# HGRN2 and GLA input blocks in pairs through DRAM, more gate blocks in the mixers, z gates multiplied in the branch stage

## The chip, the cores and the metric

The kernel runs on one core of one Trainium2 chip. The metric is the device time of one execution in microseconds; of the kernel before three runs were timed, and one more execution was profiled. Five engines work side by side: TensorE (PE, with its weight loads PEld), VectorE (DVE), ScalarE (ACT), GpSimd (POOL) and SyncE (SP), which here issues the DMAs.

## The reference

One layer of a hybrid recurrent decoder for 1024 prompt tokens, 16 meta tokens ahead of them, and 8 samples of 4 tokens: 1072 tokens in all, 1056 without the meta tokens.

```python
xn = rmsnorm(h, norm_w)
(gq, gk, gv, glr, gg, hq, hf, hi, hg_g, mq, mk, mv, mi, mf, mo, mg,
 ca, cb, cg, mgate) = split_cols(xn @ w_in)
...
zA = head_rmsnorm(oA, gla_norm) * jax.nn.silu(gg)
...
zB = head_rmsnorm(oB, hg_norm) * jax.nn.silu(hg_g)
...
zC = head_layernorm(hC, ml_norm) * jax.nn.silu(mg)
...
zD = jax.nn.silu(yc32) * jax.nn.silu(cg)
gates = jax.nn.sigmoid(mgate).reshape(Bsz, T, 4, D_MODEL)
mixed = gates[:, :, 0] * (zA @ w_branch[0])
...
h = h + mixed @ w_out
```

`oA` comes from gated linear attention, `oB` from HGRN2 (q is silu(hq), the forget gate f comes from hf, k is 1 - f, v is hi), `hC` from an mLSTM, `yc32` from a causal depthwise convolution over 31 taps and a LayerNorm; `mixed` is the sum over the four branches, and a final RMSNorm ends it. `xn @ w_in` has 1024 input channels and is cut into blocks of 128 output columns; `mgate` alone has 32 of them. Each matrix product is made of three in a shorter format: both operands are split into a high and a low part (`xh`, `xl`, `wh`, `wl`), and high by high, low by high and high by low are added.

## The kernel before, in words

**Stages, with their place in the profiled execution.** Up to about 90 us: the input norm, transposes into `xh` and `xl`, four direct gate blocks (`NDIR`). 90 to 501: the pair stage. 501 to 1300: the mixers, four HGRN2 units (`hg_unit`), two GLA units of two heads each (`gla_unit`) and four mLSTM units (`ml_unit`). 1300 to 1323: two late gate blocks (`LATE`). 1323 to 1517: the branch stage. To the end: `w_out` and the final norm.

**A direct block** (`proj`, `proj_w`, L185 to L187) multiplies one block of 128 columns by all tokens: three groups of tokens (352 wide each without the meta tokens, `GY`; 358, 358 and 356 with them, `GA`), 24 matmuls a group, 72 in all, into an accumulator `acc` from a ring of three. Its weights are loaded by SP (`load_raw`, `wraw`, 512 KB), rounded by ACT into `wh` and subtracted by POOL into `wl` (`split_w`, L138 and L139).

**A pair** (`pair`, L277 to L279) makes two blocks by seven half products in place of eight: the sums and differences of the weights are made on DVE (`ta`, `tb`, L261 to L267), as are two of the splits; the products `sa`, `sb`, `sc`, `sd`, 168 matmuls 268 wide, are added up on ACT and DVE in `p1`, `u2`, `p5` and `u3` (L289 to L310). `pair_to` writes the two blocks to DRAM, after a sigmoid or a silu where one is wanted. The stage has 19 pairs: four that make the conv input (`conv_pair`), and 15 of `todo`: five of gate blocks, two of `cg`, and the eight of `mo`, `gg`, `hg` and `mg`. Each conv pair's 30 taps (`y`, L388) run on DVE under the pairs behind it.

**The mixers** make their own inputs by direct blocks: `hf`, `hq`, `hi` (L185 within `hg_unit`, `vtok`), `gk`, `gq`, `gv`, `mq`, `mk`, `mv`. A unit transposes `v` to tokens (`tta`, `v9p`), makes the decays level by level (`lv`, `tot`), the states (`ds`, `sall`), the outputs (`op`), and in `z_out` transposes the normed output (`zt`) and multiplies it by the norm's weight and the z gate (L720, DVE), which was loaded into `gt` from `sscr`. Sixteen gate blocks (`fill`) are made directly between: two in each HGRN2 unit, one in each GLA unit, one each in three mLSTM units and three in the last.

**The branch stage** takes the branches in the order 1, 0, 2, 3. `load_z` loads four `zr` and splits them on ACT and DVE into `zh` and `zl` (L1149, L1150). For each of eight column blocks `j` the weights `w_br` are loaded and split, 36 matmuls go into three accumulators, DVE multiplies by the gate `gt` and POOL adds to `mix` (L1164, L1165).

**What sets the order.** A list scheduler orders each engine's instructions ahead of time. Each engine goes through its list in order, and so does SP with the DMA issues: an issue that waits for a buffer or for data holds all behind it. Buffers are rings by tag; a tile waits for the readers of the one that it replaces. Pools are opened and closed by stage, so a mixers' tile lies where the pair stage's tiles lay.

Of the kernel before, what the change touches and what calls it, by code (L numbers as in the profile page):

```python
# [65 lines left out]
def trunk(ctx, tc, hx, w_in, w_sm, w_br, w_out, pk, wgk2, mlb, fnorm, s_gla, s_hg, s_c, s_n, s_m, s_cv,  # L66
# [246 lines left out]
    def pair_to(sec, i, dst, func, times=False, base=0):  # L313
# [5 lines left out]
        def c11(s, ps):  # L319
# [4 lines left out]
            if s == 1:  # L324
                DMA.dma_start(dst[i, :, 0:HT - NM], g11[:, NM:])

        def rest(j, second):
            def ev(t):
# [6 lines left out]
                if second:  # L335
                    DMA.dma_start(dst[j, :, HT - NM:], t)
# [233 lines left out]
    def vtok(sec, i, ones_col=False):  # L570
# [4 lines left out]
        def ev(ps, t0, n):  # L575
            S.activation(vf[:, t0:t0 + n], ps, AF.Copy)
# [125 lines left out]
    def z_out(o, rstd, nw, gate, zi, mu=None):  # L702
# [9 lines left out]
        for c0, c1 in QUADS:  # L712
# [7 lines left out]
            V.scalar_tensor_tensor(gate[:, t0:t0 + e - a], ps[:, a:e], nw, gate[:, t0:t0 + e - a], ALU.mult, ALU.mult)  # L720
# [100 lines left out]
    def gla_unit(p):  # L821
# [11 lines left out]
        def ev(ps, t0, n):
            V.tensor_tensor(prod[:, t0:t0 + n], ps, k[:, t0:t0 + n], ALU.mult)
            for i, r in ((0, slice(0, 64)), (1, slice(64, 128))):
                V.tensor_tensor(qg[r, i, t0:t0 + n], ps[r], f[r, t0:t0 + n], ALU.mult)
# [5 lines left out]
        gates = []
        for i in range(2):
            g = tl("gt", [P, NY], 2)
            DMA.dma_start(g, sscr[2 * p + i])
            gates.append(g)
# [486 lines left out]
```

## Time and profile before

| | |
|---|---|
| median of three runs | 1619.72 us (1619.08 to 1622.87) |
| the profiled execution | 1622.92 us |
| its span, from the first to the last instruction | 1621.1 us |
| mean granted clock of TensorE | 0.993 |
| bytes moved by DMA | 176 MB |

A row of the page or of a group gives the line, the engine, the operation, the tile written and those read, the shape and the count; behind the first bar the busy time in us and the mean ns of one; behind the second the idle time just before these instructions and what ended it. A row of the timeline gives start and duration in us, and in brackets the idle time ahead of it and what released it. SPq rows are the issues of DMAs, not the transfers. A row of DMA issues ends with KB and the median us from issue to landing. A row of waits gives the total us, the number and the longest.

### The profile page before, as it was taken

The numbers are of one execution on the slowest core, as the hardware profiler recorded it, in microseconds if no ns is written. First come the engines' busy times: TensorE is split into PE (matmuls) and PEld (weight loads), VectorE is DVE, ScalarE is ACT, GpSimd is POOL, SyncE is SP. The second block draws the span as 40 slices with busy tenths as digits, with TensorE's granted clock in tenths as the row PEclk, the third lists the DMA queues.
The fourth block names the chain that finished last, engine by engine and source line by source line (L and its number), as shares of the span: only waits on it lengthen the run. The fifth ranks groups of instructions, "written<-read, shape, count | busy, mean of one in ns | idle before, by whom it ended". The sixth has DMA issues, their size and how long they took to land.

```text
span 1621.1 us, 27103 instructions
## 1 busy us (share of the span) xinstructions
PE 1582.3 (98%) x10894; PEld 1529.0 (94%) x10894; DVE 1076.6 (66%) x1900; ACT 527.4 (33%) x1015; POOL 467.0 (29%) x412
## 2 busy tenths in 40 slices
PE   7999999899999999999999999999999999999998
PEld 6999999899999999999999998999999999999886
DVE  7959979899994566454544766585864736744523
ACT  6533342333333333212423212133322235522311
POOL 2222222123223122222122322123322312777300
PEclk9999999999999999999999999999999999999999
DMA  5323333232336213131313123143432277676221
GB/s 195 126 75 110 96 105 87 77 103 84 109 99 200 58 38 106 42 101 47 102 46 106 40 68 104 45 147 109 130 96 70 94 222 231 191 232 205 87 105 58
DMA packets 190561, 176.21 MB, mean 109 GB/s; under 512 B 9260, under 2 KB 164800, under 8 KB 190436
## 3 DMA queue, kind: packets, MB, share of 16 engines
q1 hardware_dynamic: 190436, 174.49, 35.1%
q8 instruction: 85, 1.39, 0.4%
q14 instruction: 40, 0.33, 0.1%
HBM read 122.45 MB, written 52.00 MB: 108 GB/s over the span
## 4 chain that ended last, share of the span: by engine, by line
PE 80%; DVE 14%; DMA 2%; issue 2%; ACT 1%; SPq 0%; DVEq 0%; POOLq 0%; POOL 0%; ACTq 0%
PE acc L185 17%; PE acc L187 17%; PE acc L186 17%; DVE y L388 5%; PE lv L627 4%; PE sa L277 2%; PE sa L278 2%; PE sa L279 2%; PE sc L279 1%; PE sc L278 1%; PE sc L277 1%; PE sd L279 1%; PE sd L278 1%; PE sd L277 1%; DVE wl L139 1%
## 5 line engine op out<-in xcount | busy, mean ns | idle before, releaser
L139 POOL TENSOR_TENSOR wl<-wraw,wh 128x1024 fp32r<-128x1024 f32 (+1 forms) x124 | 272.1, 2196 | 680.4 <-ACT wh L138 671.6
L185 PE MATMUL acc<-xh,wh 128*128 128x352 f32 (+2 forms) x1320 | 435.8, 330 | 2.9 <-ACT vt L534 1.9
L186 PE MATMUL acc<-xl,wh 128*128 128x352 f32 (+2 forms) x1320 | 434.3, 329 | 0.0
L187 PE MATMUL acc<-xh,wl 128*128 128x352 f32 (+2 forms) x1320 | 433.5, 328 | 0.0
L185 PEld LDWEIGHTS acc<-xh,wh 128*128 128x128 f32 x1320 | 249.9, 189 | 6.9 <-ACT vt L534 2.9
L186 PEld LDWEIGHTS acc<-xl,wh 128*128 128x128 f32 x1320 | 249.8, 189 | 2.0 <-issue 0.5
L187 PEld LDWEIGHTS acc<-xh,wl 128*128 128x128 f32 x1320 | 249.7, 189 | 1.7 <-issue 0.2
L138 ACT ACTIVATE wh<-wraw 128x512 fp32r<-128x512 f32 (+1 forms) x125 | 110.5, 884 | 253.7 <-PE acc L186 147.7
L388 DVE SCALAR_TENSOR_TENSOR y<-u,pkt,y 128x1024 f32<-128x1024 f32 x120 | 190.8, 1590 | 0.7
L185 PE MATMUL acc<-zh,wh 128*128 128x352 f32 x384 | 124.5, 324 | 0.5 <-DVE gt L1164 0.4
L186 PE MATMUL acc<-zl,wh 128*128 128x352 f32 x384 | 124.3, 324 | 0.0
L187 PE MATMUL acc<-zh,wl 128*128 128x352 f32 x384 | 124.2, 323 | 0.0
L277 PE MATMUL sa<-xh,wh 128*128 128x268 f32 x304 | 89.0, 293 | 6.5 <-ACT u L349 6.1
L642 DVE TENSOR_TENSOR q<-q,tot 128x256 f32<-128x256 f32 (+3 forms) x96 | 59.4, 619 | 53.9 <-PE lv L627 42.6
L278 PE MATMUL sa<-xl,wh 128*128 128x268 f32 x304 | 88.2, 290 | 0.0
L279 PE MATMUL sa<-xh,wl 128*128 128x268 f32 x304 | 88.1, 290 | 0.0
L1165 POOL TENSOR_TENSOR mix<-mix,gt 128x352 f32<-128x352 f32 x72 | 72.1, 1014 | 30.4 <-DVE gt L1164 25.1
L627 PE MATMUL lv<-q,k 128*128 128x128 f32 (+2 forms) x608 | 74.5, 272 | 2.7 <-DVE att L660 2.5
L627 PEld LDWEIGHTS lv<-q,k 128*128 128x128 f32 (+1 forms) x608 | 71.0, 187 | 4.7 <-issue 3.9
L185 PEld LDWEIGHTS acc<-zh,wh 128*128 128x128 f32 x384 | 72.3, 188 | 1.1 <-DVE gt L1164 1.1
L187 PEld LDWEIGHTS acc<-zh,wl 128*128 128x128 f32 x384 | 72.2, 188 | 0.0
L186 PEld LDWEIGHTS acc<-zl,wh 128*128 128x128 f32 x384 | 72.2, 188 | 0.0
(391 smaller groups left out, 3392.9 us busy)
## 6 DMA issues: line engine op xcount, KB each, us to landing
wraw<-w_in SPq DMA_DIRECT2D x92, 512.0 KB, 4.0
gt<-gscr SPq DMA_DIRECT2D x30, 528.0 KB, 5.0
gscr<-gd SPq DMA_DIRECT2D x60, 176.0 KB, 1.9
zr<-zscr SPq DMA_DIRECT2D x16, 528.0 KB
wraw<-w_br SPq DMA_DIRECT2D x32, 256.0 KB, 2.9
gt<-sscr SPq DMA_DIRECT2D x12, 528.0 KB, 3.6
zscr<-gt SPq DMA_DIRECT2D x12, 528.0 KB, 3.3
sscr<-u SPq DMA_DIRECT2D x16, 268.0 KB, 2.3
```

Of the source, the lines that this page charges most:

```text
L138: S.activation(hi[:, :kd], raw[:, :kd], AF.Copy)
L139: (E or G).tensor_tensor(lo[:, :kd], raw[:, :kd], hi[:, :kd], ALU.subtract)
L185: T.matmul(ps, wh(k), ah(k), start=(i == 0), stop=False)
L186: T.matmul(ps, wh(k), al(k), start=False, stop=False)
L187: T.matmul(ps, wl(k), ah(k), start=False, stop=(i == kd - 1))
L277: T.matmul(out, wh, xa[:, k], start=start and k == 0, stop=False, skip_group_check=True)
L278: T.matmul(out, wh, xb[:, k], start=False, stop=False, skip_group_check=True)
L279: T.matmul(out, wl, xa[:, k], start=False, stop=stop and k == KH - 1, skip_group_check=True)
L388: V.scalar_tensor_tensor(ymain, u[:, NM + j:NM + j + NPR], w(j), ymain, ALU.mult, ALU.add)
L627: T.matmul(out(ps[:rows, c], P), k[:, t0:t0 + rows], moving(t0, P), start=True, stop=True)
L642: V.tensor_tensor(qx[:, :, 1], qx[:, :, 1], pv[r, :, 0:1].broadcast_to([rw, nb, h]), ALU.mult)
L1165: G.tensor_tensor(mixed[j][:, t0:t0 + n], mixed[j][:, t0:t0 + n], gt[:, t0:t0 + n], ALU.add)
```

## The change

The 12 blocks of HGRN2 and the 8 of GLA become ten pairs, which write to a new DRAM buffer `pscr`; the units load them back (`take`). The five gate pairs go, and their ten blocks join the fillers: 26 of them, four in every HGRN2 and GLA unit, two in the last mLSTM unit. The loop over the conv pairs takes four pairs of `todo` for each in place of three. `z_out` no longer knows the gate: ACT scales the transposed output by the norm's weight and stores it in pieces, and `load_z` loads the z gate `zg` (one buffer) and multiplies on DVE. `tot` and `sall` get second buffers, and the fillers' output shares `zst` with `z_out`. The raw weights have one buffer in the working pool in place of two; the second raw block of a pair lies in the pair stage's own pool.

```diff
+    pscr = dr.tile([20, P, NT], F32, name="pscr", tag="pscr")
-    def load_raw(src, c0, kd=KD):
-        raw = pools["wp"].tile([P, KD, P], F32, name="wraw", tag="wraw")
+    def load_raw(src, c0, kd=KD, pool="wp"):
+        raw = pools[pool].tile([P, KD, P], F32, name="wraw", tag="wraw", bufs=1)
...
-        r0, r1 = load_raw(w_in, c0), load_raw(w_in, c1)
+        r0, r1 = load_raw(w_in, c0), load_raw(w_in, c1, pool="gph")
...
-    NFILL = 16
-    fill = list(range(32 - NFILL, 32))
-    todo = [("gate", i, gscr, AF.Sigmoid) for i in range(NDIR, 32 - NFILL, 2) if i not in LATE]
+    fill = [j for j in range(NDIR, 32) if j not in LATE]
+    PB, todo, nb = {}, [], 0
+    for sec, n in (("hf", 4), ("hq", 4), ("hi", 4), ("gk", 2), ("gq", 2), ("gv", 4)):
+        PB[sec] = nb
+        todo += [(sec, i, pscr, AF.Copy, False, nb, 0) for i in range(0, n, 2)]
+        nb += n
...
-        pair_to(*todo.pop(0))
+        n = (3, 3, 3, 3)[i]
+        for t in todo[:n]:
+            pair_to(*t)
+        del todo[:n]
...
+    def take(sec, i, dst, lead=0):
+        DMA.dma_start(dst, pscr[PB[sec] + i, :, lead:])
...
-        proj(sec, i, GA, ev)
+        if sec in PB:
+            take(sec, i, vf[:, :NT])
+        else:
+            proj(sec, i, GA, copy_evac(vf))
+        S.activation(x9, vf[:, NP:NT].unsqueeze(1).broadcast_to([P, 3, NT - NP]), AF.Copy)
...
-        tot = tl("tot", [P, 1072], 1)
+        tot = tl("tot", [P, 1072], 2)
...
-            V.scalar_tensor_tensor(gate[:, t0:t0 + e - a], ps[:, a:e], nw, gate[:, t0:t0 + e - a], ALU.mult, ALU.mult)
-        DMA.dma_start(zscr[zi], gate)
+            z = tl("zst", [P, 512], 2)[:, :e - a]
+            S.activation(z, ps[:, a:e], AF.Identity, scale=nw)
+            DMA.dma_start(zscr[zi, :, t0:t0 + e - a], z)
...
-        for _ in range(3 - nh):
+        for _ in range(4):
             filler()
...
-        sall = tl("sall", [P, 9, P], 1)
+        sall = tl("sall", [P, 9, P], 2)
...
-        proj("hf", h, GA, evf)
+        take("hf", h, k)
+        S.activation(f, k, AF.Sigmoid)
+        S.activation(k, k, AF.Sigmoid, scale=-1.0)
+        V.tensor_scalar(f, f, oml[:, h:h + 1], lbA[:, h:h + 1], ALU.mult, ALU.add)
+        V.tensor_scalar(k, k, oml[:, h:h + 1], kb[:, h:h + 1], ALU.mult, ALU.subtract)
         G.memset(q[:, 0:NM], 0.0)
-        proj("hq", h, GY, silu_evac(q))
+        take("hq", h, q[:, NM:], NM)
+        S.activation(q2[:, 1, NM:], q[:, NM:], AF.Sigmoid)
+        V.tensor_tensor(q[:, NM:], q[:, NM:], q2[:, 1, NM:], ALU.mult)
...
-        for _ in range(3 if h == 3 else 1):
+        for _ in range(2 if h == 3 else 0):
             filler()
...
             zr = ztl("zr", 2)
             DMA.dma_start(zr, zscr[4 * b + k])
+            if b < 3:
+                zg = ztl("zg", 1)
+                DMA.dma_start(zg, sscr[4 * b + k])
+                V.tensor_tensor(zr, zr, zg, ALU.mult)
```

**The order on PE between the pair stage and the mixers.** Before: the last product of the last pair (`sd`), then the first direct block, of HGRN2's `hf`.

```order
L277 MATMUL sd_5465<-xh_96,wh_5339 128x268
L278 MATMUL sd_5465<-xl_97,wh_5339 128x268
L279 MATMUL sd_5465<-xh_96,wl_5340 128x268
L185 MATMUL acc_5623<-xh_96,wh_5619 128x358
L186 MATMUL acc_5623<-xl_97,wh_5619 128x358
L187 MATMUL acc_5623<-xh_96,wl_5620 128x358
```

Nine groups of 24 such matmuls stand there before the first `tta`. In the change:

```order
L278 MATMUL sd_6586<-xh_97,wh_6460 128x268
L279 MATMUL sd_6586<-xl_98,wh_6460 128x268
L280 MATMUL sd_6586<-xh_97,wl_6461 128x268
L540 MATMUL tta_6755<-ident_70,vf_6749 128x128 x4
L540 MATMUL tta_6761<-ident_70,vf_6749 128x128 x4
L540 MATMUL tta_6767<-ident_70,vf_6749 48x128
L555 MATMUL v9p_6770<-ident_70,x9_6751 96x128
L186 MATMUL acc_6928<-xh_97,wh_6924 128x352
L187 MATMUL acc_6928<-xl_98,wh_6924 128x352
```

The transposes of `vf`, which is loaded from `pscr`, are next behind the pair; the first direct block, a filler, comes behind them.

**The order on SP at the same place.** Before, the last pair's stores (`u3`, `p1`, `u2`) and what follows them:

```order
L336 DMA sscr_91<-u3_5408 128x536
L338 DMA sscr_91<-p1_5353 128x520
L132 DMA wraw_6058<-w_in 128x8x128
L336 DMA sscr_91<-u2_5354 128x536
L479 DMA lvf_5576<-c_lvl 128x640
L480 DMA lvf_5576<-c_lvt 48x168
L872 DMA gt_5909<-sscr_91 128x1056
L874 DMA s0_5911<-s_hg 128x8x128
```

In the change:

```order
L133 DMA wraw_7012<-w_in 128x8x128
L390 DMA yscr_93<-y_5675 128x1056
L133 DMA wraw_7102<-w_in 128x8x128
L337 DMA sscr_91<-u3_6529 128x536
L339 DMA sscr_91<-p1_6474 128x520
L337 DMA sscr_91<-u2_6475 128x536
L486 DMA lvf_6697<-c_lvl 128x640
L487 DMA lvf_6697<-c_lvt 48x168
L549 DMA k_6736<-pscr_92 128x1072
L549 DMA q_6737<-pscr_92 128x1056
L549 DMA vf_6749<-pscr_92 128x1072
```

The loads of `k`, `q` and `vf` are new behind the stores, and a second raw weight load stands ahead of them.

**The order on SP at the start of the branch stage.** Before, the loads of z for the first branch (`zr_13192` to `zr_13210`), conv rows `yc`, weights and a gate:

```order
L1144 DMA zr_13192<-zscr_85 128x1056
L1144 DMA zr_13198<-zscr_85 128x1056
L1113 DMA yc_13219<-yscr_92 128x4x128
L1114 DMA yc_13219<-cscr_89 128x4x128
L1144 DMA zr_13204<-zscr_85 128x1056
L1144 DMA zr_13210<-zscr_85 128x1056
L132 DMA wraw_13440<-w_br 128x4x128
L1200 DMA gt_13438<-gscr_88 128x1056
```

In the change:

```order
L1135 DMA zr_13559<-zscr_85 128x1056
L1138 DMA zg_13561<-sscr_91 128x1056
L1135 DMA zr_13568<-zscr_85 128x1056
L1104 DMA yc_13598<-yscr_93 128x4x128
L1105 DMA yc_13598<-cscr_89 128x4x128
L1195 DMA gt_13829<-gscr_88 128x1056
L1138 DMA zg_13570<-sscr_91 128x1056
L1135 DMA zr_13577<-zscr_85 128x1056
L1138 DMA zg_13579<-sscr_91 128x1056
L1104 DMA yc_13679<-yscr_93 128x4x128
L1105 DMA yc_13679<-cscr_89 128x4x128
L133 DMA wraw_13831<-w_br 128x4x128
```

Between the loads of `zr` stand those of `zg`, and the second branch weight and the last `zr` come behind them. On PE, 144 gate matmuls stand between the last `zt` and the first matmul of the branches before, 89 in the change.

More of the change, by code (lines that the diff above doesn't have):

```diff
@@ L324, in c11 @@
             if s == 1:
-                DMA.dma_start(dst[i, :, 0:HT - NM], g11[:, NM:])
+                DMA.dma_start(dst[i, :, 0:HT - lead], g11[:, lead:])
         def rest(j, second):
@@ L335, in ev @@
                 if second:
-                    DMA.dma_start(dst[j, :, HT - NM:], t)
+                    DMA.dma_start(dst[j, :, HT - lead:], t)
                 else:
-                    DMA.dma_start(dst[j, :, 0:HT - NM], t[:, NM:])
+                    DMA.dma_start(dst[j, :, 0:HT - lead], t[:, lead:])
             return ev
@@ L700, in vblk_for, with z_out @@
         return vb
-    def z_out(o, rstd, nw, gate, zi, mu=None):
+    def z_out(o, rstd, nw, zi, mu=None):
         if mu is not None:
@@ L829, in gla_unit @@
         k = tl("k", bufs=2)
-        proj("gk", p, GA, copy_evac(k))
+        take("gk", p, k)
         prod = tl("prod", bufs=1)
[L833 to L836, printed above, removed]
         G.memset(qg[:, :, 0:NM], 0.0)
         G.memset(prod[:, 0:NM], 0.0)
-        proj("gq", p, GY, ev)
+        take("gq", p, prod[:, NM:], NM)
+        for i, r in ((0, slice(0, 64)), (1, slice(64, 128))):
+            V.tensor_tensor(qg[r, i, NM:], prod[r, NM:], f[r, NM:], ALU.mult)
+        V.tensor_tensor(prod[:, NM:], prod[:, NM:], k[:, NM:], ALU.mult)
         vts = [vtok("gv", 2 * p + i) for i in range(2)]
[L842 to L846, printed above, removed]
         s0 = tl("s0", [P, NSEQ, 129], 1)[:, :, 0:P]
@@ L870, in hg_unit @@
         vt = vtok("hi", h)
-        g = tl("gt", [P, NY], 2)
-        DMA.dma_start(g, sscr[4 + h])
         s0 = tl("s0", [P, NSEQ, 129], 1)[:, :, 0:P]
@@ L901, in ml_rows @@
         s84 = lambda t: t[:, NP:NT].rearrange("p (s j) -> p s j", j=NDEC)
-        b = row("b", "sall", 1)[0:4]
+        b = row("b", "sall", 2)[0:4]
         segm = tl("prod", [4, NT], 1, name="segm")
@@ L970, in ml_unit @@
         to_tok_v(sf, so)
-        g = tl("gt", [P, NY], 2)
-        DMA.dma_start(g, sscr[8 + h])
         c0t = tl("s0", [P, NSEQ, 129], 1, name="c0t")
@@ L979, in ml_unit @@
         DMA.dma_start(inb, rscr[4 + h:5 + h].broadcast_to([P, NT]))
-        dm = tl("sall", [P, 9, 129], 1, name="dm")[:, 0:8, 0:P]
+        dm = tl("sall", [P, 9, 129], 2, name="dm")[:, 0:8, 0:P]
         dmt = tl("dmt", [TAIL, TAIL], 1)
@@ L986, in ml_unit @@
         S.activation(dmt, dmt, AF.Exp)
-        sd = tl("tot", [P, 8, P], 1, name="sd")
+        sd = tl("tot", [P, 8, P], 2, name="sd")
         for c0, c1 in QUADS[:2]:
@@ L1005, in ml_unit @@
         k9 = split3(xk, 2, "k9", 1, mmt("k9p"), cols9[:, h:h + 1])
-        call = tl("sall", [P, 9, 129], 1, name="call")
+        call = tl("sall", [P, 9, 129], 2, name="call")
         for a in range(0, 9, 3):
@@ L1062, in ml_unit @@
         G.memset(ms, 1.0)
-        sq = tl("sall", [P, 9, P], 1, name="sq")
+        sq = tl("sall", [P, 9, P], 2, name="sq")
         for n, c1, c2 in ((P, 0, 8), (TAIL, 8, 9)):
```

27 lines of the change are left out of this document (6 added, 21 removed).

## The prediction

> **What bounds the kernel now.** I read the page first: its head, the busy shares and the chain that ended last.
>
> ```profile
> span 1621.1 us, 27103 instructions
> PE 1582.3 (98%) x10894; PEld 1529.0 (94%) x10894; DVE 1076.6 (66%) x1900; ACT 527.4 (33%) x1015; POOL 467.0 (29%) x412
> PE 80%; DVE 14%; DMA 2%; issue 2%; ACT 1%; SPq 0%; DVEq 0%; POOLq 0%; POOL 0%; ACTq 0%
> ```
>
> TensorE is busy for 98% of the span, so a change pays by the matmul time that it takes away and costs by every hole that it opens. VectorE has 14% of the chain, and the windows by stage say where (the columns are the window, its length, then busy time and count of PE, PEld, DVE, ACT and POOL, the granted clock, the DMA share and GB/s).
>
> ```profile
> 89.80:500.60 410.80, 401.54 (x3213) 399.15 (x3212) 374.61 (x448) 148.66 (x282) 102.96 (x46) 0.99 0.34 101
> 500.60:1060.00 559.40, 550.70 (x3885) 533.30 (x3884) 315.08 (x677) 151.68 (x274) 140.72 (x145) 0.99 0.25 73
> 1060.00:1300.00 240.00, 239.46 (x1579) 232.65 (x1578) 157.59 (x411) 74.05 (x174) 70.94 (x73) 1.00 0.35 107
> 1323.40:1517.00 193.60, 192.83 (x1220) 191.44 (x1219) 112.17 (x178) 77.33 (x146) 118.38 (x111) 1.00 0.65 200
> 320.00:360.00 40.00, 40.00 (x326) 40.00 (x326) 39.89 (x41) 15.17 (x29) 9.41 (x4) 1.00 0.35 108
> ```
>
> The first row is the pair stage: VectorE is busy for 374.61 of 410.80 us, and in the last row, 40 us inside that stage, for 39.89 of 40: PE and DVE are both full there. In the mixers (second and third row) DVE has 473 of 799 us, in the branch stage (fourth) less than 60%; there PE alone bounds.
>
> Third, the PE timeline where it stands still, and the granted clock behind two such places.
>
> ```profile
> 195.24 0.39 PE L277 MATMUL sa<-xh,wh 128*128 128x268 f32 x1 [1.23 <-ACT u L349]
> 297.82 0.59 PE L277 MATMUL sa<-xh,wh 128*128 128x268 f32 x1 [4.85 <-ACT u L349]
> 972.65 0.79 PE L817 MATMUL sds<-vb,k 96*128 96x512 f32 x1 [2.14 <-DVE gt L720]
> ```
>
> ```profile
> 296.70:303.50 6.80, 5.68 (x25) 5.62 (x26) 4.14 (x10) 1.34 (x4) 0.84 (x2) 0.50 0.51 157
> 972.60:976.00 3.40, 3.35 (x11) 3.25 (x12) 3.37 (x7) 0.00 (x0) 0.00 (x0) 0.51 0.98 308
> ```
>
> A stop of 4.85 us is followed by 6.8 us at half clock, one of 2.14 us by 3.4 us at half clock. So a stop costs its length and some 1.7 to 3.4 us more.
>
> **The change part by part.** The sum is made against the profiled execution, 1622.92 us (span 1621.1 and 1.8 around it), 3.2 above the median of the three runs, 1619.72.
>
> *Matmul work: -15.2.* The pair stage passes 326 matmuls 268 wide in 40 us, 0.1227 us each; the 168 of a pair take 20.6, and with the few small transposes beside them I use 20.75. A direct block is three groups of 24 matmuls; two of the late gates' groups are evacuated one behind the other:
>
> ```profile
> 1303.98 0.46 ACT L214 ACTIVATE gt<-acc 128x352 f32<-128x352 f32 x1 [3.95 <-PE acc L187]
> 1307.85 0.47 ACT L214 ACTIVATE gt<-acc 128x352 f32<-128x352 f32 x1 [3.41 <-PE acc L187]
> ```
>
> 3.87 us a group, 11.6 a block 352 wide, by width 11.8 a block 358 wide. The 20 direct blocks of HGRN2 and GLA (14 wide ones, 6 of 352) are 235.4 us and become 10 pairs, 207.5: -27.9. Five gate pairs (103.75) become 10 direct gate blocks (116.4): +12.65.
>
> *Stalls of the pair stage: -13 (-17 to -4).* 19 pairs at 20.75 are 394 us of the stage's 410.8: 17 us are stops, the largest the one at 297.82, where `sa` waits for `u`, and VectorE is busy with conv taps ahead of it. VectorE's costs of a pair, grouped over that stage:
>
> ```profile
> L388 DVE SCALAR_TENSOR_TENSOR y<-u,pkt,y 128x1024 f32<-128x1024 f32 x120 | 190.8, 1590 | 0.7
> L139 DVE TENSOR_TENSOR wl<-ta,wh 128x1024 fp32r<-128x1024 f32 x18 | 21.9, 1218 | 1.2 <-ACT wh L138 1.0
> L301 DVE TENSOR_TENSOR u<-u,p 128x536 f32<-128x536 f32 x19 | 17.5, 919 | 11.0 <-ACT u L300 11.0
> L306 DVE TENSOR_TENSOR p<-u,sc 128x268 f32<-128x268 f32 x38 | 16.0, 423 | 1.5 <-PE sc L279 1.5
> L261 DVE TENSOR_TENSOR ta<-wraw 128x512 f32<-128x512 f32 x18 | 12.3, 686 | 9.1 <-issue 6.5 <-DMA wraw<-w_in 2.5
> ```
>
> Two splits (2 x 1.218), four differences (4 x 0.686), two whole adds (2 x 0.919), six half adds (6 x 0.423) are 9.6 us a pair. The five pairs more have no sigmoid and no multiply, so DVE gets 374.6 + 5 x 9.6 = 423 us in 24 x 20.75 = 498: 85% where it was 91%, and each conv pair has four others behind it in place of three, so its 31 taps are through before the next conv pair wants DVE. I take 13 of the 17 us. The last conv's taps run on into the last four pairs, which keeps a few us; below, only the 4.85 us stop may go.
>
> *Seam from the pair stage to the mixers: +16 (12 to 22).* Before, PE passes it without a stop, because direct blocks need nothing but weights:
>
> ```profile
> 480.00:510.00 30.00, 30.00 (x226) 30.00 (x226) 18.36 (x31) 11.13 (x21) 8.56 (x12) 1.00 0.86 274
> 502.83 0.72 DVE L332 TENSOR_TENSOR u<-u,sg 128x536 f32<-128x536 f32 x1 [0.78 <-ACT sg L331]
> 503.58 0.92 SPq L336 DMA_DIRECT2D sscr<-u  x1
> 504.59 0.39 SPq L479 DMA_DIRECT2D lvf<-c_lvl  x1
> 505.51 0.42 SPq L872 DMA_DIRECT2D gt<-sscr  x1
> gt<-sscr SPq DMA_DIRECT2D x12, 528.0 KB, 3.6
> ```
>
> After, the first PE rows behind the last `sd` are transposes of `vf`, which SP fetches fifth behind the last pair's store `u2` (the two orders are in the section on the change). The last product ends at 500.6; SP issues that store 3.0 us later and is done with it at 3.9; two `lvf` loads, `k`, `q` and `vf` follow at about 0.45 each, so `vf` is asked for at about 6. One load of that size lands in 3.6 alone: 10 us. The five together are some 2.5 MB, 9 us at this place's 274 GB/s: 13. And a raw weight load now stands ahead of the three last stores and waits for POOL to be done with the only buffer. I take 13.5 us of stop and 2.5 for the half clock; the low end is 10 and 2, the high end 18 and 4. Nothing of the gates can step in: all groups use one ring of accumulators in program order, and the filler comes behind `v9p`.
>
> *Seam from the mixers to the branches: +10 (5 to 13).* Before, two late gates (23.3 us) lie between the last `zt` and the first branch matmul, and four loads of z fit in:
>
> ```profile
> 1299.21 1.57 DVE L720 SCALAR_TENSOR_TENSOR gt<-zt,pkt,gt 128x496 f32<-128x496 f32 x3 [4.22 <-PE zt L716]
> 1304.56 0.86 SPq L1144 DMA_DIRECT2D zr<-zscr  x2
> 1308.35 1.09 ACT L1149 ACTIVATE zh<-zr 128x1056 fp32r<-128x1056 f32 x1
> 1317.97 1.26 DVE L1150 TENSOR_TENSOR zl<-zr,zh 128x1056 fp32r<-128x1056 f32 x1 [1.26 <-ACT zh L1149]
> ```
>
> From the evacuation of `zt` at 1299.2 to the end of the last `zl` at 1319.2 it is 20.0 us. After, PE's order has only 89 gate matmuls there, 89 x 0.161 = 14.4 us, and SP's order puts four `zg` loads between the `zr`, into one buffer: each waits for the multiply of the one before. A step is a landing of 3.6 (the row of `gt<-sscr`, the same data) and a multiply of about 1.1, which I take from the subtraction of that shape, 1.26, as near. Four steps from 1304.56, then `zh` 1.09 and `zl` 1.26: the last `zl` is 5.4 + 4 x 4.7 + 2.4 = 26.6 us behind `zt`. PE wants it some 4 to 5 us into its first block, 14.4 + 4.8 = 19.2. That leaves 7.4, and 2.5 for the clock, since PE stops piecewise, k by k. The row at 972.65 has half clock after only 2.14 us. The Trainium skill, "TensorE: Matmul & The Clock Gate", section "What's actually happening", has the clock halved after an idle window of about 3.4 us; by that rule pieces of 2 to 3 us would stay at full clock, and the term would be +7.5. The trace's row does not agree with it, and decides.
>
> *Branch stage: +4 (0 to 8 within the forecast).* Its weights now have one raw buffer.
>
> ```profile
> wraw<-w_br SPq DMA_DIRECT2D x32, 256.0 KB, 2.9
> L138 ACT ACTIVATE wh<-wraw 128x512 fp32r<-128x512 f32 x31 | 19.5, 628 | 52.2 <-PE acc L186 32.1 <-POOL mix L1165 13.1 <-POOL wl L139 2.8
> L139 POOL TENSOR_TENSOR wl<-wraw,wh 128x512 fp32r<-128x512 f32 x31 | 42.8, 1380 | 37.7 <-ACT wh L138 37.7
> L1165 POOL TENSOR_TENSOR mix<-mix,gt 128x352 f32<-128x352 f32 x71 | 70.2, 1002 | 29.4 <-DVE gt L1164 24.1 <-DVE vc L1125 3.6 <-PE acc L187 1.7
> ```
>
> Issue about 0.4, landing 2.9, 0.63 and 1.38 are 5.3 us a block, one after another; PE takes 36 x 0.161 = 5.8. It fits by half a microsecond, so I put +2 on it; and +2 on `gt` and raw loads that stand in SP's queue behind `zg` loads waiting for DVE. The 12 `zg` loads are bytes (6.5 MB) that moved here from the mixers; the queue share of 0.65 holds them.
>
> *Mixers: +5 (-3 to 15).* PE loses 20 blocks and gains 10 there, so a unit has less to lie under its chains. The stops in this stage now:
>
> ```profile
> PE lv L627 <- DVE att L660: 2.5, 3, 1.7
> PE sds L817 <- DVE gt L720: 2.1, 1, 2.1
> PE tta L533 <- ACT vf L576: 1.9, 1, 1.9
> ```
>
> 6.5 us. The gates per linear unit rise to four, always at the levels; where no filler stands (between `ds` and `op`) a few new stops are likely. Second buffers for `tot` and `sall`, and the z multiply gone from DVE, work the other way. DVE has 473 us against some 680 of PE: it doesn't become the bound. I take +5.
>
> Sum: -15.2 - 13 + 16 + 10 + 4 + 5 = +6.8 on 1622.92; from the median, 1626.
>
> **The rivals.**
>
> *Cheap seams, faster (0.30).* If `vf` lands by the single-load row (10 us of stop, 2 of clock), the z loads run ahead (5), and the mixers and branches take nothing, the sum is -28.2 + 17 = -11: 1609. For it: the pair stage's gain is matmul work and sure; against it: both orders on SP. It decides where the two seams together cost under 23.
>
> *The raw buffer bounds the branches (0.13).* With a POOL `mix` (1.0 us) ahead of `wl`, or loads of 4 rather than 2.9 us at a DMA share of 0.65, a block takes 6.7 in place of 5.8: 0.9 x 24 = 21, in place of the 2 above: 1645. For it: the margin of 0.5 us; against it: the DMA landing row is from that busy stage itself.
>
> *Chains of the mixers come bare (0.12).* One stop per linear unit as that at 972.65, 2.14 + 1.7 = 3.8; with six units 23 in place of 5: 1644. For it: fewer blocks per unit; against it: the levels keep their full cover.
>
> That the change might not do what it says can be left out: the orders show the pairs, the loads and the fillers.
>
> **How the numbers follow.** The forecast, 1626 (its own range 1618 to 1634), has 0.45. The rivals have 0.30, 0.13 and 0.12. A measurement can tell about 0.3%, 4.9 us: faster is below 1614.9, slower above 1624.6. Faster: 0.28 of the first rival. Within: 0.02 of it and 0.18 of the forecast's lower half. Slower: 0.27 of the forecast and 0.25 of the others, 0.52. The range goes from 1606, into the first rival, to 1645, to the other two; about 0.1 is left out on each side.
>
> **What would show it.** Right: the pair stage ends near 89.8 + 24 x 20.75 + 4 = 592; PE stops once for 10 us or more before the first `tta`, released by the load of `vf`, with a clock near 0.5 after it; the first branch block's matmuls wait for `zl`; steps of 4 to 5 us between the multiplies of `zr`. Wrong: no stop of 8 us at the first seam, or late gates that still cover the z loads; a branch block that takes over 6 us (the second rival); many stops of 2 us before `op` or `zt` (the third); a pair stage over 605 us, which would mean that the taps' stalls stay.

## The result and the profile after

The changed kernel takes 1683.30 us (median of four runs, 1678.43 to 1689.19), the kernel before beside it 1620.56: ratio 1.0387, 95% interval 1.035 to 1.0425. The forecast, 1626 with a range to 1645, had the sign and a tenth of the size. Its profiled execution, the slowest of the four and 5.9 above their median, took 1689.19 us; its span is 1686.3, 65.2 more than before. One slip first: the section on the change, and a step of the prediction, say that the loop takes four other pairs behind each conv pair. It takes five, two single ones and three of the slice: a cycle is six pairs long, where it was four.

The page of the changed kernel: head, busy shares, chain.

```profile
span 1686.3 us, 27713 instructions
PE 1595.3 (95%) x11014; PEld 1534.3 (91%) x11014; DVE 1100.6 (65%) x1910; ACT 555.4 (33%) x1057; POOL 457.8 (27%) x412
PE 75%; DVE 11%; DMA 8%; ACT 2%; issue 2%; POOL 1%; SPq 1%; DVEq 0%; POOLq 0%; ACTq 0%
```

TensorE's share falls from 98% to 95%, and DMA has 8% of the chain where it had 2%. TensorE's busy time rises by 13 us, though its work at full clock is smaller: more of it runs at half clock. The windows by stage (the same columns as before), cut at the first and last matmul of each: start, pair stage, the stop at the first seam, mixers up to the last `zt`, late gates, branch stage, tail.

```profile
0.00:93.90 93.90, 77.75 (x441) 72.40 (x441) 71.30 (x117) 51.59 (x90) 23.67 (x28) 0.96 0.48 152
93.90:593.80 499.90, 499.86 (x4052) 499.56 (x4050) 412.91 (x510) 173.46 (x324) 112.26 (x55) 1.00 0.34 102
593.80:612.80 19.00, 0.00 (x0) 0.02 (x1) 11.34 (x17) 5.51 (x7) 6.54 (x10) 0.62 0.74 242
612.80:1348.80 736.00, 703.22 (x4795) 675.95 (x4795) 434.82 (x1009) 222.42 (x441) 186.19 (x197) 0.96 0.31 93
1348.80:1364.80 16.00, 15.15 (x96) 14.80 (x95) 2.48 (x3) 4.80 (x10) 1.28 (x1) 1.00 0.71 234
1364.80:1582.90 218.10, 203.16 (x1223) 195.48 (x1222) 127.87 (x193) 80.64 (x149) 121.09 (x111) 0.97 0.68 216
1582.90:1686.30 103.40, 96.20 (x417) 76.13 (x415) 39.85 (x65) 16.97 (x40) 6.80 (x10) 0.99 0.25 89
```

The pair stage is now full, 499.86 of 499.90 us busy, without a stop: 24 pairs at 20.83. The mixers' row is the bad one: 32.8 us idle, and a clock of 0.96. The trace's record of the granted clock, summed over that stage, has 53.9 us at half clock (before: 6.8), 6.1 of them behind the first seam's stop. The mixers of the kernel before, cut in the same way, are idle for 9.2 us:

```profile
535.50:1299.80 764.30, 755.06 (x5246) 730.84 (x5244) 461.04 (x1064) 218.16 (x434) 202.07 (x204) 1.00 0.27 82
```

Against the same stages of before:

| stage | before | after | difference | forecast |
|---|---|---|---|---|
| start, to the first pair | 89.8 | 93.9 | +4.1 | 0 |
| pair stage | 410.8 | 499.9 | +89.1 | +90.8 (five pairs more, -13) |
| seam, mixers, late gates, to the first branch matmul | 822.8 | 771.0 | -51.8 | -98 (-235.4 + 116.4 + 16 + 5) |
| branch stage | 194.4 | 218.1 | +23.7 | +14 |
| tail | 103.3 | 103.4 | +0.1 | 0 |
| sum | 1621.1 | 1686.3 | +65.2 | +6.8 |

**First seam.** The timeline of the changed kernel, SP's issues and the first PE instruction behind the last pair:

```profile
598.23 0.33 SPq L390 DMA_DIRECT2D yscr<-y  x1
600.43 0.38 SPq L133 DMA_DIRECT2D wraw<-w_in  x1
602.44 0.32 SPq L337 DMA_DIRECT2D sscr<-u  x1
605.65 0.34 SPq L549 DMA_DIRECT2D k<-pscr  x1
606.57 0.38 SPq L549 DMA_DIRECT2D vf<-pscr  x1
612.81 0.66 PE L540 MATMUL tta<-ident,vf 128*128 128x128 f32 x2 [19.05 <-DVE tot L601]
```

The last product ends at 593.8. SP waits for the last conv taps (`yscr`, 598.2), then for POOL to free the only raw buffer (600.4), and asks for `vf` at 606.6; it lands 6.0 us later. The releaser in brackets is not the cause: `tot` is only DVE's last event before the load came (in e4, below, the same stop of 19.19 us is put down to the load of `vf` itself). The stop has 19.05 us, and the 6.1 us at half clock behind it cost 3 more.

**Mixers.** The waits of PE and ACT that name `zst`, the two buffers that the fillers and `z_out` share:

```profile
PE acc L186 <- ACT zst L218: 5.8, 3, 2.3
PE n0p L947 <- ACT zst L723: 3.2, 1, 3.2
PE tt L540 <- ACT zst L723: 1.8, 1, 1.8
PE sds L820 <- ACT zst L723: 1.6, 3, 0.5
ACT zst L723 <- DMA zscr<-zst: 14.7, 9, 2.3
```

And one such place in the timeline, at the end of the second HGRN2 unit:

```profile
789.28 1.24 ACT L723 ACTIVATE zst<-zt,pkt 128x496 f32<-128x496 f32 x2
792.10 0.30 ACT L723 ACTIVATE zst<-zt,pkt 128x48 f32<-128x48 f32 x1 [1.58 <-DMA zscr<-zst]
792.75 0.46 ACT L218 ACTIVATE zst<-acc 128x352 f32<-128x352 f32 x1 [0.35 <-DMA zscr<-zst]
793.26 0.66 PE L186 MATMUL acc<-xh,wh 128*128 128x352 f32 x1 [1.71 <-ACT zst L218]
```

The window behind it:

```profile
794.10:797.30 3.20, 3.20 (x15) 3.20 (x14) 2.05 (x5) 2.38 (x3) 0.00 (x0) 0.64 1.07 329
```

`z_out` makes three pieces into two buffers, so the third waits in ScalarE for the store of the first; behind it in ScalarE's list stands the evacuation of a filler, and the filler's next group has no accumulator. That path was not in the prediction. It explains 12.4 us of the 32.8; the others are waits for the chains' own steps on DVE, ACT and the loads. Four of these rows:

```profile
PE lvt L633 <- DVE k L645: 3.3, 2, 1.8
PE lvt L633 <- DVE att L662: 3.0, 1, 3.0
PE sds L820 <- DVE vb L700: 2.4, 2, 1.4
PE op L789 <- DVE sall L776: 2.0, 2, 1.0
```

**Branch stage.** DVE's multiplies by `zg` in the timeline, and PE waiting behind them:

```profile
1361.45 1.26 DVE L1139 TENSOR_TENSOR zr<-zr,zg 128x1056 f32<-128x1056 f32 x1 [9.29 <-DMA zg<-sscr]
1367.17 1.26 DVE L1139 TENSOR_TENSOR zr<-zr,zg 128x1056 f32<-128x1056 f32 x1 [2.05 <-DMA zg<-sscr]
1372.17 1.26 DVE L1139 TENSOR_TENSOR zr<-zr,zg 128x1056 f32<-128x1056 f32 x1 [1.28 <-DMA zg<-sscr]
1377.66 1.26 DVE L1139 TENSOR_TENSOR zr<-zr,zg 128x1056 f32<-128x1056 f32 x1 [0.60 <-DMA zg<-sscr]
1369.60 0.75 PE L186 MATMUL acc<-zh,wh 128*128 128x352 f32 x2 [2.86 <-ACT zh L1144]
```

And the window behind them:

```profile
1371.00:1381.00 10.00, 7.10 (x23) 5.71 (x23) 4.72 (x6) 3.78 (x10) 0.56 (x1) 0.55 0.85 271
```

The steps are 5.7, 5.0 and 5.5 us (forecast 4.7), and after the piecewise stops the clock is down for 10 us.

### The profile page after: what moved, and what is told of

Its sections match the earlier page's. It is cut to its first block, busy times and chain, and to the rows that moved or that the text cites. A ratio compares the mean times of both kernels' runs of the same rounds, so it can differ in the third digit from the quotient of the medians.

```text
span 1686.3 us, 27713 instructions
## 1 busy us (share of the span) xinstructions
PE 1595.3 (95%) x11014; PEld 1534.3 (91%) x11014; DVE 1100.6 (65%) x1910; ACT 555.4 (33%) x1057; POOL 457.8 (27%) x412
## 4 chain that ended last, share of the span: by engine, by line
PE 75%; DVE 11%; DMA 8%; ACT 2%; issue 2%; POOL 1%; SPq 1%; DVEq 0%; POOLq 0%; ACTq 0%
PE acc L186 12%; PE acc L187 12%; PE acc L188 12%; PE lv L629 3%; PE sa L279 3%; PE sa L278 3%; PE sa L280 3%; PE sc L280 3%; PE sc L279 2%; PE sc L278 2%; PE sd L280 2%; PE sd L279 2%; PE sd L278 2%; DVE y L389 2%; PE sb L278 1%
## 5 line engine op out<-in xcount | busy, mean ns | idle before, releaser
L186 PE MATMUL acc<-xh,wh 128*128 128x352 f32 (+2 forms) x1080 | 365.6, 339 | 8.4 <-ACT zst L218 5.8
L187 PE MATMUL acc<-xl,wh 128*128 128x352 f32 (+2 forms) x1080 | 362.9, 336 | 0.0
L188 PE MATMUL acc<-xh,wl 128*128 128x352 f32 (+2 forms) x1080 | 362.2, 336 | 0.0
L186 PEld LDWEIGHTS acc<-xh,wh 128*128 128x128 f32 x1080 | 210.7, 195 | 12.2 <-ACT zst L218 6.2
L187 PEld LDWEIGHTS acc<-xl,wh 128*128 128x128 f32 x1080 | 210.8, 195 | 1.9 <-issue 0.4
L188 PEld LDWEIGHTS acc<-xh,wl 128*128 128x128 f32 x1080 | 210.3, 195 | 1.9 <-issue 0.4
L278 PE MATMUL sa<-xh,wh 128*128 128x268 f32 x384 | 110.4, 288 | 0.0
L279 PE MATMUL sa<-xl,wh 128*128 128x268 f32 x384 | 110.2, 287 | 0.0
L280 PE MATMUL sa<-xh,wl 128*128 128x268 f32 x384 | 110.1, 287 | 0.0
L218 ACT ACTIVATE zst<-acc 128x352 f32<-128x352 f32 x78 | 35.6, 460 | 167.3 <-PE acc L188 101.7
L186 PEld LDWEIGHTS acc<-zh,wh 128*128 128x128 f32 x384 | 72.6, 190 | 13.5 <-ACT zh L1144 7.9
```

The costliest lines, as they stand in the source:

```text
L186: T.matmul(ps, wh(k), ah(k), start=(i == 0), stop=False)
L187: T.matmul(ps, wh(k), al(k), start=False, stop=False)
L188: T.matmul(ps, wl(k), ah(k), start=False, stop=(i == kd - 1))
L278: T.matmul(out, wh, xa[:, k], start=start and k == 0, stop=False, skip_group_check=True)
L279: T.matmul(out, wh, xb[:, k], start=False, stop=False, skip_group_check=True)
L280: T.matmul(out, wl, xa[:, k], start=False, stop=stop and k == KH - 1, skip_group_check=True)
```

## The experiments

All times are medians with the ratio to the kernel before on the same chip, and its 95% interval in brackets. Theory A: rings and queues (`zst`, `zg`, the raw buffer) make the stops. Theory B: the mixers' chains have too little matmul work over them.

**e1 and e2: more zst buffers.** Memory has room for four only with one `tot`, so e1 is the control.

```diff
-        tot = tl("tot", [P, 1072], 2)
+        tot = tl("tot", [P, 1072], 1)
```

> The changed kernel with one buffer for tot again (this only makes room for the next experiment, and is its control). Theory A (ScalarE is held by the two zst buffers, whose stores must land first, and holds TensorE's accumulators) and theory B (the mixers' chains have too little matmul work over them, the rings don't matter) both expect the time of the changed kernel, 1683 us within 6, since no stop of its trace names tot.

1679.24 us, ratio 1.0337 (1.0320 to 1.0355): not measurably slower than the change; the second `tot` brings nothing here. Then, beside that edit:

```diff
-            z = tl("zst", [P, 512], 2)[:, :e - a]
+            z = tl("zst", [P, 512], 4)[:, :e - a]
-        gate_direct(fill.pop(0), tmp=lambda: tl("zst", [P, 512], 2))
+        gate_direct(fill.pop(0), tmp=lambda: tl("zst", [P, 512], 4))
```

> The same as e1, with four zst buffers in place of two. Theory A: the 12.4 us in which TensorE waits for ScalarE's zst in the mixers go, and six stretches of half clock with them: 18 to 28 us faster than e1, about 1660. Theory B: the stops move to the next wait of the chain, under 6 us faster than e1.

1667.25, ratio 1.0267 (1.0251 to 1.0282): 12 us faster than e1, between the two theories. The mixers' windows of e1 and of e2:

```profile
613.30:1337.80 724.50, 694.91 (x4795) 667.86 (x4795) 438.25 (x1009) 221.47 (x440) 191.54 (x197) 0.97 0.31 94
```

```profile
612.40:1329.50 717.10, 692.01 (x4791) 663.71 (x4791) 439.89 (x1009) 221.94 (x442) 188.36 (x197) 0.98 0.32 95
```

Idle time falls only from 29.6 to 25.1, though the waits that name `zst` fell from 13.8 to 5.3: other waits of the chains took half of their place. The mixers are 7.4 us shorter; 7.0 us more come in the branch stage (220.8 to 213.8), whose cause was not traced. The ring is a real cause, and not the main one.

**e3: two fillers ahead of the first unit.**

```diff
+    FILLS = [3, 3, 4, 4, 4, 4]
+    filler()
+    filler()
     hg_unit(0)
...
-        for _ in range(4):
+        for _ in range(FILLS.pop(0)):
```

> The changed kernel with two of the 26 filler blocks made before the first HGRN2 unit (the first two units make three each in place of four). If the 19.05 us stop at the first seam is only the load of vf behind the last stores, two blocks (23.3 us) cover it and its half clock: 18 to 23 us faster than the changed kernel, about 1662. Rival: the first two units miss these blocks and open stops of their own, and the gain is under 10 us.

1677.22, ratio 1.0329 (1.0313 to 1.0345): 6 us below the change by the medians, some 9 by the ratios. Its windows from the last pair to the first `tta`, and of the mixers:

```profile
593.90:621.00 27.10, 24.80 (x144) 24.51 (x144) 16.67 (x23) 8.51 (x13) 9.60 (x12) 0.94 0.75 240
621.00:1339.00 718.00, 681.37 (x4653) 653.27 (x4650) 435.05 (x1003) 215.86 (x432) 186.54 (x196) 0.96 0.31 93
```

The stop is gone (2.3 us left of 19), so it was the load of `vf`; but the mixers have 36.6 us idle where they had 32.8, and 58 us at half clock. Blocks taken from over the chains opened stops there: the rival's figure, and a first sign for theory B.

**e4: z gates in the mixers again.**

```diff
+            V.scalar_tensor_tensor(gate[:, t0:t0 + e - a], ps[:, a:e], nw, gate[:, t0:t0 + e - a], ALU.mult, ALU.mult)
+        DMA.dma_start(zscr[zi], gate)
...
-            if b < 3:
-                zg = ztl("zg", 1)
-                DMA.dma_start(zg, sscr[4 * b + k])
-                V.tensor_tensor(zr, zr, zg, ALU.mult)
```

> The z gates loaded and multiplied in the mixers again, as before the change (one buffer for tot and sall, the fillers' own gd), pairs, fillers and the single raw buffer as in the change. Theory A and the theory that the zg loads hold the branch stage: mixers some 20 us shorter, branch stage at 195 to 200 us in place of 219, sum 1683 - 42 = about 1641. Rival C (the single raw buffer holds the branch stage): the branch stage stays at 210 us or more, about 1655. Theory B: the mixers keep their length, about 1660.

1660.43, ratio 1.0222 (1.0207 to 1.0237). Mixers and branch stage:

```profile
613.70:1334.60 720.90, 691.54 (x4811) 663.58 (x4811) 440.99 (x1044) 207.02 (x411) 188.44 (x198) 0.99 0.34 104
1348.20:1555.50 207.30, 198.34 (x1224) 193.31 (x1223) 112.77 (x180) 80.14 (x149) 120.03 (x111) 0.99 0.64 198
```

Against the change, 11 us came back in the branch stage and 15 in the mixers, there nearly all through the clock: the mixers' idle time is still 29.4. Against e1, which has the same single `tot`, the branch stage is 13.5 us shorter and the mixers only 3.6. Theory A's 42 us were too many; 1660 was theory B's figure.

**e5: the second raw buffer back.**

```diff
-        raw = pools[pool].tile([P, KD, P], F32, name="wraw", tag="wraw", bufs=1)
+        raw = pools[pool].tile([P, KD, P], F32, name="wraw", tag="wraw", bufs=2)
...
-        r0, r1 = load_raw(w_in, c0), load_raw(w_in, c1, pool="gph")
+        r0, r1 = load_raw(w_in, c0), load_raw(w_in, c1)
```

> e4 with the second raw weight buffer back in the working pool, so what is left of the change are the ten pairs through DRAM and the 26 fillers. If the single raw buffer holds the branch stage (its 207 us in e4 against 194 before) and the first stage (94.6 against 89.8), both go back: 1660 - 12 - 4 = about 1644. If the branch stage's rest is a seam cost of the z loads with only 89 gate matmuls over them, it gives 4 to 6 us: about 1655.

1654.77, ratio 1.0215 (1.0194 to 1.0236). Start, mixers and branch stage:

```profile
0.00:89.40 89.40, 75.56 (x440) 70.05 (x441) 71.16 (x117) 51.29 (x90) 23.35 (x28) 0.96 0.50 160
609.00:1333.20 724.20, 694.24 (x4811) 665.23 (x4811) 445.57 (x1043) 208.97 (x412) 188.85 (x198) 0.99 0.33 103
1345.50:1548.50 203.00, 197.22 (x1224) 194.27 (x1223) 115.42 (x180) 80.55 (x149) 120.54 (x111) 0.98 0.66 205
```

The start is as before (89.4), so its +4.1 was the single buffer. The branch stage goes from 207.3 to 203.0; the rest of its excess stays, as the second forecast had it. In the ratios e5 stands hardly below e4. With rings and buffers as before the change, pairs and fillers alone still cost 2%.

**e6 and e10: fillers moved.** e6 is e5 with the edit of e3.

> e5 with two of the fillers made ahead of the first HGRN2 unit (three in each of the first two units). The stop at the first seam (19.2 us and its half clock) is covered by 23.3 us of blocks; in e3 half of that was given back in the mixers as the zst stops grew. With those stops gone, 14 to 20 us faster than e5. Rival: the first two units need these blocks, and again under 10 us are gained.

1642.67, ratio 1.0142 (1.0124 to 1.0161): 12 us faster than e5, between the two figures; the mixers still have 31.8 us idle. e10 spreads the fillers evenly:

```diff
-    FILLS = [3, 3, 4, 4, 4, 4]
+    FILLS = [2, 3, 3, 3, 4, 4]
...
-        for _ in range(2 if h == 3 else 0):
+        for _ in range(2 if h == 3 else 1):
```

> e6 with its 26 fillers spread in another way: two ahead, then 2, 3, 3, 3 in the HGRN2 units, 4 and 4 in the GLA units, and 1, 1, 1, 2 in the mLSTM units (e6: two ahead, 3, 3, 4, 4, 4, 4 and 0, 0, 0, 2). If the stops are missing work over the chains, the ones of the mLSTM units (v9p and zt, about 10 us) shrink and the HGRN2 units stay covered: 6 to 12 us faster than e6, 1632 to 1637. If all units together have too little work, stops only move: within 4 us of e6.

1646.93, ratio 1.0156 (1.0140 to 1.0172): no gain. 29.6 us idle and 41 at half clock: stops only moved. All units together have too little to lie under.

**e7: the ten pairs and nothing else.**

```diff
-    fill = [j for j in range(NDIR, 32) if j not in LATE]
-    PB, todo, nb = {}, [], 0
+    fill = list(range(32 - NFILL, 32))
+    PB, nb = {}, 0
+    todo = [("gate", i, gscr, AF.Sigmoid) for i in range(NDIR, 32 - NFILL, 2) if i not in LATE]
...
-        for _ in range(4):
+        for _ in range(3 - nh):
```

> The kernel before with the ten pairs through DRAM and nothing else: 16 fillers, the five gate pairs, z gates and raw buffers as before. Matmul work 27.9 us under the kernel before, pair stage 5 pairs longer than the change's and without its own stops as in the change, the first seam's 22 us stop. Theory B (the mixers live from the work over their chains, and the pairs take 20 blocks of it): the mixers open over 40 us of stops, result 1640 to 1670. Rival (cover is enough): 1624 - 28 - 17 + 23 + 5 = about 1607.

1692.20, ratio 1.0447 (1.0428 to 1.0465): beyond theory B's 1670 and slower than the change itself, with 12.65 us less matmul work than e5. Its mixers:

```profile
706.60:1370.30 663.70, 610.09 (x4071) 577.01 (x4071) 447.43 (x1044) 188.24 (x372) 162.52 (x187) 0.91 0.31 96
```

53.6 us idle, the clock at 0.91 (114.7 us at half clock). The ten more fillers of the change were needed to hold the mixers up at all. Its first seam is also of use: here ten pairs follow the last conv pair, its taps are stored at 588.7 us, over 100 us ahead of the seam, and the stop is 12.64 us in place of 19.05.

```profile
706.59 0.66 PE L542 MATMUL tta<-ident,vf 128*128 128x128 f32 x2 [12.64 <-DVE tot L603]
```

**e8 and e11: fewer blocks in pairs.** e8 makes `v` (hi and gv) directly again; e11 leaves GLA direct, and its fillers are `FILLS = [3, 3, 4, 4, 2, 2]`, two ahead of the first unit and 1, 1, 1, 3 in the mLSTM units. The edit of e8:

```diff
-    for sec, n in (("hf", 4), ("hq", 4), ("hi", 4), ("gk", 2), ("gq", 2), ("gv", 4)):
+    for sec, n in (("hf", 4), ("hq", 4), ("gk", 2), ("gq", 2)):
...
-        n = (3, 3, 3, 3)[i]
+        n = (2, 2, 2, 2)[i]
```

> e5 with the v blocks (hi and gv, eight) direct again, only hf, hq, gk and gq in six pairs through DRAM; 26 fillers, so the mixers hold 34 direct blocks beside those of the mLSTM, about the 36 of before. The first unit starts on a direct block. If the cost is the lost cover at the seam and over the chains, both come back: matmul work -16 + 12.7, pair stage without stops -17, no seam stop: 1624 - 20 = about 1604 (1598 to 1612). If loading k and q from DRAM itself costs (waits for their landing in every unit), 1620 or more.

> Only the 12 blocks of HGRN2 in six pairs; GLA's eight blocks direct as before; 26 fillers, two of them ahead of the first unit, then 3, 3, 4, 4, in GLA 2 and 2, in the mLSTM units 1, 1, 1, 3; z gates and raw buffers as before. As many direct blocks in the mixers as e8 (34 beside the mLSTM's), with the first seam covered. By the cover theory: matmul work -3.4, pair stage -7, seam +5, mixers +5, branches +4: 1620 to 1628. If DRAM loads of HGRN2's inputs cost by themselves: over 1635.

1632.45, ratio 1.0074 (1.0058 to 1.0090), and 1634.13, ratio 1.0076 (1.0059 to 1.0094). Both come most of the way back, neither reaches the kernel before. Theory B's figure for e8, about 1604, was missed by 28 us, and its rival's bound was met; e11 lies between its two. Pair stage and mixers of e8:

```profile
89.00:510.20 421.20, 417.94 (x3382) 417.00 (x3380) 370.56 (x448) 148.21 (x277) 93.12 (x48) 1.00 0.34 102
523.40:1310.00 786.60, 766.47 (x5299) 738.79 (x5299) 466.28 (x1051) 223.55 (x439) 215.47 (x214) 0.99 0.33 98
```

With cycles of five pairs, 3.3 us of stops are left in the pair stage, and the last taps run over its end: of the 20 us idle in e8's mixers 10.2 lie in the first 35 us, where SP asks for `k` and `q` only behind the store of those taps. In the other 751.6 us the mixers are idle for 10.0, about as the kernel before, so the loads of `k` and `q` do not cost in every unit. With a pair stage some 6 us over its forecast and a branch stage 5.3 us over that of before, this is most of the 28 us.

**e13: more cover, and nothing else.** Eight fillers of e5 are computed twice.

```diff
+    fill += fill[:8]
...
-        for _ in range(4):
+        for _ in range(FILLS.pop(0)):
+    FILLS = [4, 4, 4, 4, 6, 6]
...
-        for _ in range(2 if h == 3 else 0):
+        for _ in range(3 if h == 3 else 1):
```

> e5 with eight filler blocks computed a second time (the same gates written again), so that the GLA units have six each and the mLSTM units 1, 1, 1 and 3: 42 direct blocks in the mixers beside the mLSTM's own in place of 34 less. Nothing else changes: the same loads from DRAM, the same pairs. Eight blocks are 8 x 11.65 = 93 us of matmul work. If missing cover makes the stops (some 30 us idle and 22 us at half clock in e5), 15 to 28 us of them go and the time is e5 plus 65 to 78: 1720 to 1733. If the loads from DRAM or ScalarE's order make them, the time is e5 plus 90 to 95: 1745 to 1750.

(The counts of blocks in that text are wrong: it is 34 direct blocks beside the mLSTM's own, in place of 26.) 1723.37, ratio 1.0616 (1.0598 to 1.0633): 68.6 us above e5 for 93 us of matmul work. Mixers, late gates and branch stage:

```profile
609.30:1399.80 790.50, 772.86 (x5316) 746.54 (x5316) 451.12 (x1043) 233.39 (x447) 208.43 (x205) 0.99 0.34 104
1399.80:1423.50 23.70, 23.70 (x151) 23.62 (x150) 6.33 (x8) 7.61 (x12) 3.66 (x2) 1.00 0.76 243
1423.50:1618.50 195.00, 193.86 (x1224) 192.13 (x1222) 112.38 (x178) 77.48 (x146) 119.73 (x111) 1.00 0.66 200
```

24 us of e5's loss are gone with the same loads and pairs, as theory B had it: 12 us of idle time in the mixers, and 8 in the branch stage, which is back at 195.0, now that 23.7 us of late gates lie over the loads of z; e5 had 12.3.

Ten of e5's 30 us idle were stops behind the loads of `vf` (`v9p` behind ScalarE's copy `x` of it 6.8, `tta` 3.4), and 1 of them is left in e13: here a load from DRAM cost time where no matmuls lay over it. ScalarE's waits for the one store buffer of the fillers, `gd`, grow from 38.1 to 42.8 us meanwhile, so they are not what stops PE.

The series, idle time and time at half clock of the mixers from the first `tta` to the last `zt`, by direct blocks there beside the twelve of the mLSTM (counted in the traces, 72 matmuls a block; three blocks of the kernel before stand ahead of its first `tta`):

| kernel | direct blocks | idle, us | at half clock, us |
|---|---|---|---|
| e7 | 17 | 53.6 | 114.7 |
| e5 | 27 | 29.9 | 21.2 |
| e13 | 34 | 17.6 | 20.0 |
| e8 (eight of them v) | 34 | 20.1 | 10.2 |
| before | 33 | 9.2 | 6.8 |

From e7 to e13 the idle time falls as blocks are added. The number of blocks is not all: with 33 the kernel before has half of e13's idle time, and the time at half clock does not follow the count from e5 to e13. What makes that difference was not tested.

**e9, e12 and e14: the pair stage's stops by themselves.** These are the kernel before with other pairs between the conv pairs. e9:

```diff
         conv_states(i, *cu)
         pair_to(*todo.pop(0))
+        if i < 3:
+            pair_to(*todo.pop(0))
```

> The kernel before, with four in place of three other pairs behind each of the first three conv pairs (the three that stood at the end come forward; nothing else moves). If the pair stage's stops are the conv taps that DVE has not finished when the next conv pair's tile is wanted, a cycle of five pairs (104 us) has room for them, the stop of 4.85 us and its half clock go, and the last taps run on under the direct blocks of the first unit: pair stage 400 in place of 410.8 us, time 1608 to 1614 against 1621. If the changed kernel lost its stops only because its new pairs ask less of DVE, nothing changes, 1621.

1633.47, ratio 1.0072 (1.0058 to 1.0086). The pair stage, and PE behind it:

```profile
88.80:491.20 402.40, 398.43 (x3215) 397.69 (x3214) 351.51 (x425) 148.17 (x280) 93.98 (x46) 1.00 0.33 100
```

```profile
532.31 0.67 PE L185 MATMUL acc<-xh,wh 128*128 128x358 f32 x1 [13.78 <-DVE q L542]
```

The stage is 8.4 us shorter, as expected; then the first unit's evacuations stand on DVE behind the last taps, 13.8 us are lost, and the time misses its forecast by 20 us. e12 has the extra pair only behind the second conv pair:

```diff
+        if i == 1:
+            pair_to(*todo.pop(0))
```

> The kernel before with one pair moved: the second conv pair has four others behind it, the last keeps five (3, 4, 3, 5 in place of 3, 3, 3, 6). In e9 the pair stage's stops halved, but the last conv's taps ran over its end and held the next stage for 13.8 us. Here the last conv keeps six pairs in all, so nothing should run over, and the stop of 4.85 us in front of the third conv pair with its 6.8 us at half clock should go: 8 us faster than the kernel before, 1612 to 1615. If the stop only moves to the fourth conv pair: within 3 us of the kernel before.

1624.45, ratio 1.0010 (0.9999 to 1.0021): no change. The stop moved to the fourth conv pair and grew:

```profile
410.74 0.59 PE L277 MATMUL sa<-xh,wh 128*128 128x268 f32 x1 [7.49 <-ACT u L349]
```

e14 is e9 with two fillers ahead of the first unit:

```diff
+    FILLS = [1, 1, 2, 2, 1, 1]
+    filler()
+    filler()
     hg_unit(0)
...
-        for _ in range(3 - nh):
+        for _ in range(FILLS.pop(0)):
```

> e9 (the kernel before with four other pairs behind each of the first three conv pairs) with two filler blocks ahead of the first HGRN2 unit, which with the second makes one in place of two. The pair stage keeps its 402 us. If the 13.8 us stop of e9 is the first unit's own work queued behind the conv taps on DVE, blocks that only ScalarE evacuates cover it: 1610 to 1615. If SP's wait for the store of the taps holds the fillers' stores and weights too, the stop stays: 1628 to 1634.

1639.80, ratio 1.0102 (1.0085 to 1.0118): the rival's mechanism, 6 us beyond its range. The fillers' store stands in SP's list behind the store of the taps, and ScalarE waits for it:

```profile
526.09 0.46 ACT L217 ACTIVATE gd<-acc 128x352 f32<-128x352 f32 x1 [21.34 <-DMA gscr<-gd]
```

No version tried beats the kernel before.

## Why the prediction failed, point by point

- **Matmul work, -15.2: held within some 4 us.** The pair stage runs 24 pairs at 20.83 us, the figure used was 20.75. An estimate from the traces, PE's busy time less half of what lies in stretches at half clock, is 10.9 us below the kernel before in the change, 12.8 in e5 and 25.0 in e7 (27.9 by its blocks); e13 is 90.9 above e5 (93 by its blocks).
- **Pair stage, -13 (-17 to -4): right mechanism, -15 measured.** All stops went; at 20.83 us a pair they were 15 us, not the 17 that 20.75 gives. The taps were the cause, but the room came from cycles of six pairs, not from the five that I had read in the loop: with five (e8, e9, e11) 3 to 4 us stay, with four there is a stop of 5 to 7.5 us (before, e12).
- **First seam, +16 (12 to 22): right mechanism, somewhat small.** 22 us. The store of the taps at the head of SP's queue was not priced, and the load took 6.0 us, not 3.6. Without that store ahead, in e7, the stop is 12.64 us, near the 13.5 of the sum. One of its bounds was also wrongly reckoned: the five loads are 2.0 MB by the shapes in the order, not 2.5, which at 274 GB/s gives 11 us and not 13.
- **Second seam and branch stage, +14 together: mechanism right, 10 us small.** The steps of the `zg` chain were 5 to 5.7 us. e4 took 11 us back by undoing it, e5 some 4 more with the second raw buffer, and e13 the last 8 with full cover by late gates. The raw buffer as the bound of the stage, the second rival, did not come: e5 shows 4 us of it. Nor do its rows give its 6.7 us a block: 5.3 and 1.0 or 1.1 are 6.3 or 6.4.
- **Start, 0 forecast: +4.1.** I had looked for the single raw buffer's cost only in the branch loop. e5 takes it back.
- **Mixers, +5 (-3 to 15): this step failed.** They lost some 45 us beyond the seam. I took three rows of stops of the kernel before, 6.5 us (the whole stage has 9.2), and let them not quite double, resting on "always at the levels" for the fillers. But stops came in front of the levels too (`lvt` waits for DVE in three places, 6.3 us in all), and in front of `op`, `v9p` and `sds`. The rival "chains of the mixers come bare" had the mechanism, but counted one stop a unit at 3.8 us and got a chance of 0.12. The trace has two to five short stops in a linear unit, of 0.5 to 3 us: 32.8 us idle in the stage, and by the same estimate 22 us more lost to the clock. That lost cover makes such stops is shown by e7 and e13. On top came a new wait that the diff showed and I did not follow: fillers and `z_out` on one ring of two `zst` (12.4 us of PE's stops here; 7.4 us of the mixers' time in e2).
- **The clock.** I charged half clock to stops of 2 us, by the trace and against the rule of about 3.4 us in the Trainium skill, "TensorE: Matmul & The Clock Gate", section "What's actually happening". The changed trace bears out that shorter stops can do it: a stop of 1.71 us at 793.26 is followed by a clock of 0.64, pieces of 2.86 us and less at 1369 by 0.55 over 10 us. But not every such stop does, and the length alone does not decide. Behind this one of 1.79 us the clock stays full (the row of the stop, and the window around it):

```profile
1019.80 0.66 PE L540 MATMUL tta<-ident,vf 128*128 128x128 f32 x4 [1.79 <-DMA vf<-pscr]
1018.00:1028.00 10.00, 8.21 (x74) 8.11 (x73) 6.80 (x12) 2.24 (x5) 0.24 (x3) 1.00 0.11 33
```


What stays open: why e1, with one buffer less, has 17 us less at half clock in the mixers than the change. A difference of this size comes between executions of one kernel: the mean clocks of e1's four are 0.973 to 0.979, and 0.006 of 1677 us is 20 us at half clock. So the half-clock figures here, each of one execution, are rough. The order of instructions shifts with each edit and with it the places of short stops, so differences of 5 us between these kernels are not explained one by one.

## What to carry to other kernels

Where long dependent chains lie under independent matmuls, those matmuls are not only work: count for each stage the independent work that stays against the length of its chains, before moving a block to a place where it is 12% cheaper. Here a block of 11.8 us saved 1.4 us as half of a pair, and each of the eight blocks of e13 was worth 3 us where it stood. And a ring that two kinds of writers share, or a queue that takes issues in order, hands the wait of one to the other; follow every new tile's release to what stands behind it.
